# A decoder layer in fp32 on one core: the squares' fetches, the heads' factors, the lag of the second up product and the residual's stores change places

## The chip, the cores and the metric

The kernel runs on one core of a Trainium2 chip. The metric is the device time of one launch in microseconds (us), taken as the median of several runs. Before the change it is 1855.25 us, with runs between 1853.35 and 1856.14.

## The reference

One inference step of one layer: two SwiGLU blocks around a mixer. 1024 prompt tokens and 8 sample tokens go through the same weights; the sample tokens use caches for attention, convolution and pooling. All is fp32.

```python
h = h + 0.5 * swiglu(rmsnorm(h, g_f1), w_f1_gu, w_f1_down)
u = rmsnorm(h, g_mix) @ w_in          # q | k | v | conv value | conv gate | pool input
q, k = rmsnorm(q per head, g_q) * 64 ** -0.5, rmsnorm(k per head, g_k)
A = attention over three dilated windows (128,1), (512,4), (2048,16), merged by denominators
B = silu(layernorm(causal depthwise conv of width 31 over the GLU)) @ w_pw
C = trailing means over 2, 4, 8, 16 positions minus the token, a linear map per group
h = h + concat(A, B, C) @ w_out
h = h + 0.5 * swiglu(rmsnorm(h, g_f2), w_f2_gu, w_f2_down)
rmsnorm(x, g) = x * rsqrt(mean(x * x) + 1e-6) * g
```

## The kernel before

Everything is held transposed: D = 1024 features lie on the partitions (8 tiles of 128), T = 1032 token columns (1024 prompt and 8 sample) along the free axis, in two halves of 516 columns (`HF`, `HT`) and quarters of 258 (`QT`). An fp32 product is three TensorE matmuls: high part by high part, high by low, low by high. The high part of an operand is a rounded copy made by ScalarE (`hi`, L241), the low part is the remainder, a subtraction on VectorE (`lo`, L244) or, where the call says so, on GpSimd.

The stages follow each other: up 1 (`up`, L339), down 1, the mixer (projections, convolution, pooling, the v product, attention), `out_proj` (L897), up 2 and down 2. Instructions are placed on each engine by a scheduler that simulates a timeline (L1689), so an edit in one function can move instructions of others; within an engine the order is then fixed.

Up. Each up block is a Strassen-like scheme of seven products on halves, for each of the feature blocks `f`. The first products of `EARLY` blocks (14 in up 1, 12 in up 2) work on the raw x (operands `xo`, weights "11" and "12"), so they can run before the norm is known; their results are copied from PSUM by ScalarE (L521) and kept in DRAM (L522, `kept`). For one block `f` the product on the first half of the features ("11") runs first, and the product on the second half ("21") follows `lag` blocks later. Weights come by SP's queue (L465) into 8 buffers (`UP_WR`); temporaries of 128x516 (squares, copies, x) share 13 buffers (`UP_TMP`); the products share four PSUM buffers. Beside the first products runs a side generator: `norms()` squares the x of both halves (ScalarE, L405), adds the squares up (VectorE, L407), sums over the partitions by a matmul with a constant (L388), and takes the root and the reciprocal (L390, L391). `mixed()` then makes the operands of the other products (`xot`), with x fetched once more (L382). In up 2 the squares were already summed in `out_proj`, and `norms()` does only the last sum.

The first eight x tiles (half 0) come by SP's queue (L368); `fetch_x` brings the others: half 1 for the squares (the tiles named x_287 to x_293 and x_339 to x_345 in the order), and the tiles of `mixed()`.

The v loop (L1147 to L1169) makes v in 16 steps of 24 matmuls of 128x256. After each step it lets two side generators go on: `side_v`, which computes the heads' norm factors `rr` from sums of squares (L1198 to L1208, three chunks, each with a root on ScalarE and a reciprocal on VectorE), spreads them by a matmul (L1217, inside `norm(t)`) and scales q and k (L1218); and, inside `side_v`, `conv_tail`, which does the layer norm of the convolution, one chunk a step: split into high and low parts (low by GpSimd), mean by a matmul (`reduce`, L277), subtract (L1305). From the ninth v step on the generator `pre` begins the attention.

`out_proj` adds the mixer's product to the residual x tile by tile (L933), stores it to DRAM (`hd2`, L934) and squares it (L935). Its last steps already draw the first products of up 2, whose x is read back from `hd2`.

Of the kernel before, what the change touches and what calls it, by code (L numbers as in the profile page):

```python
# [11 lines left out]
F32 = mybir.dt.float32  # L12
# [8 lines left out]
KT = D // P  # L21
SEQ = 1024
NS = 8
T = SEQ + NS
# [4 lines left out]
HF = [slice(0, HT), slice(HT, T)]  # L29
HK = KT // 2  # L30
# [156 lines left out]
class Trunk:  # L187
# [151 lines left out]
    def up(self, src, n, g, norm, lag, extra=iter(())):  # L339
# [7 lines left out]
        nc = self.nc  # L347
# [8 lines left out]
        def tmp(name):  # L356
            return self.tmp.tile([P, HT], F32, tag="t", name=name)
# [19 lines left out]
            self.hi(X[i][:, 0, k], x)  # L377
            self.lo(X[i][:, 1, k], x, X[i][:, 0, k])

        def fetch_x(k, hf):  # L380
            x = tmp(f"x{hf}")
            nc.gpsimd.dma_start(x, src(k, hf))  # L382
            return x

        def total(hf, acc):
            ps = self.psp.tile([P, 2, 512], F32, tag="ps", name="ps")
            for j in range(2):
                nc.tensor.matmul(ps[:, j, 0:QT], self.mat[:, 1, :], acc[:, j * QT:(j + 1) * QT], start=True, stop=True)  # L388
            sd = tmp("sd")
            nc.scalar.activation(two(sd), ps[:, :, 0:QT], AF.Sqrt, bias=self.eps)  # L390
            nc.vector.reciprocal(self.r[:, HF[hf]], sd)  # L391

        def norms():
            if not norm:
                for _ in range(2):
                    yield
                total(1, self.tail)
                return
            accs = []
            xs = [fetch_x(k, 1) for k in range(HK)]  # L400
            for hf in range(2):
                acc = None
                for k in range(KT):
                    sq = xs[k] if hf else tmp("sq")
                    nc.scalar.activation(sq, sq if hf else first_x[k], AF.Square)  # L405
                    if k:
                        nc.vector.tensor_tensor(sq, sq, acc, op=ALU.add)  # L407
                    acc = sq
                    if k == HK - 1:
                        yield  # L410
                        if hf == 0:
                            xs += [fetch_x(i, 1) for i in range(HK, KT)]
                accs.append(acc)
                yield
            yield
            for hf in range(2):
                total(hf, accs[hf])
                yield
# [197 lines left out]
        def build(upto):  # L616
            nonlocal built
            while built < min(upto, len(order)):
                i, f = order[built]
                operand(f, OPERANDS[i][0])  # L620
                built += 1

        side = itertools.chain(norms(), mixed())
        load(0, True, "11")
        load_first(0)
# [224 lines left out]
    def body(self):  # L850
        nc, io, cst = self.nc, self.io, self.cst
        self.late = []
        self.mat = cst.tile([P, 3, P], F32, name="mat")
        nv = io["vec"].shape[1]
        self.vec = cst.tile([P, nv], F32, name="vec")
        self.eps = cst.tile([P, 1], F32, name="eps")
        self.r = cst.tile([P, T], F32, name="r")
        self.rel = cst.tile([33, 136], F32, name="rel")
        nc.vector.memset(self.r[:, 0:256], 0.0)
        nc.vector.memset(self.eps, EPS)  # L860
        nc.gpsimd.dma_start(self.mat, io["c_mat"])
        nc.gpsimd.dma_start(self.rel, io["rel"])
        self.gq = cst.tile([P, 1], F32, name="gq")
        self.ones = cst.tile([P, 2, P], F32R, name="ones")
        nc.gpsimd.tensor_copy(self.ones, self.mat[:, 1:3, :])
        self.mp = {i: [self.dr.tile([P, HT], F32, name=f"m{i}_{j}") for j in range(NP)]
                   for i in ("11", "21", "22", "t1", "t2", "t3", "t4")}
        hd, hd2 = [self.dr.tile([KT, P, T], F32, name=n) for n in ("hd", "hd2")]
        x0, x1 = io["x0"], io["x1"]
        self.late = []  # L870

        with self.first_pool() as self.x1p:
            gen = self.up(lambda k, hf: (x0, x1)[hf][:, k], 1, "g1", True, 1, self.toeplitz())
            while next(gen):
                pass
            with self.up_pools():
                for _ in gen:
                    pass
        with self.down_pools():
            self.down(1, lambda k, hf: (x0, x1)[hf][:, k],  # L880
                      lambda k, hf, x: nc.scalar.dma_start(hd[k][:, HF[hf]], x))
        nc.vector.tensor_scalar(self.gq, self.v("gq"), 0.125, None, op0=ALU.mult)
        with contextlib.ExitStack() as right:
            with self.page_pools():
                with self.side_pools():
                    mh, ml = self.mixer(hd)
                self.x1p = right.enter_context(self.first_pool())
                gen = self.up(lambda k, hf: hd2[k][:, HF[hf]], 2, "g2", False, 3)
                self.out_proj(mh, ml, hd, hd2, gen)
            with self.up_pools():  # L890
                for _ in gen:
                    pass
        with self.down_pools():
            self.down(2, lambda k, hf: hd2[k][:, HF[hf]],
                      lambda k, hf, x: nc.scalar.dma_start(io["yT"][k * P:(k + 1) * P, HF[hf]], x))

    def out_proj(self, mh, ml, hd, hd2, ahead):  # L897
        nc = self.nc
        steps = [(hf, d) for hf in range(2) for d in range(KT)]

        def load(at):
            hf, d = steps[at]
            raw = self.wrp.tile([P, T], F32, tag="wr", name="wr")
            hi, lo, x = self.pg("whi", F32R), self.pg("wlo", F32R), self.pg("h2")
            nc.sync.dma_start(raw[:, 0:D], self.io["wout"][d])
            nc.sync.dma_start(x[:, 0:HT], hd[d][:, HF[hf]])
            self.hi(hi[:, 0:D], raw[:, 0:D])
            self.lo(lo[:, 0:D], raw[:, 0:D], hi[:, 0:D])
            return hi, lo, x

        def total(hf, acc):
            for j in range(2):
                ps = self.ps()[:, 0:QT]
                c0 = hf * HT + j * QT
                nc.tensor.matmul(ps, self.mat[:, 1, :], acc[:, j * QT:(j + 1) * QT], start=True, stop=True)
                sd = self.pg("sd")[:, 0:QT]
                nc.scalar.activation(sd, ps, AF.Sqrt, bias=self.eps)
                nc.vector.reciprocal(self.r[:, c0:c0 + QT], sd)

        going = True  # L920
        nxt = load(0)
        for at, (hf, d) in enumerate(steps):
            hi, lo, page = nxt
            x, sq = page[:, 0:HT], page[:, HT:T]
            if at + 1 < len(steps):
                nxt = load(at + 1)
            for j in range(2):
                c = slice(hf * HT + j * QT, hf * HT + (j + 1) * QT)
                ps = self.ps()[:, 0:QT]
                self.mm3(ps, [(hi[:, k * P:(k + 1) * P], lo[:, k * P:(k + 1) * P], mh[k][:, c], ml[k][:, c])  # L930
                              for k in range(KT)])
                out = x[:, j * QT:(j + 1) * QT]
                nc.vector.tensor_tensor(out, ps, out, op=ALU.add)  # L933
            nc.gpsimd.dma_start(hd2[d][:, HF[hf]], x)  # L934
            nc.scalar.activation(sq, x, AF.Square)  # L935
            out = sq
            if hf and d == KT - 1:
                out = self.tail = self.wpage("tail")[:, 0:HT]
            if d:
                nc.gpsimd.tensor_tensor(out, sq, acc, op=ALU.add)  # L940
            acc = out
            if hf and d == 1:
                total(0, first)
            if d == KT - 1:
                first = acc
            if hf and going:
                going = next(ahead)
        while going:
            going = next(ahead)

    def mixer(self, hd):
        nc, io, cst = self.nc, self.io, self.cst
# [16 lines left out]
        src = [self.pg(f"h{k}") for k in range(KT)]  # L969
# [77 lines left out]
        for t in range(2):  # L1047
            wc = w[0]
            w = [unit(17)] if t == 0 else [unit(0), unit(4)]
            x = cx[t]  # L1050
# [13 lines left out]
        vs = self.mc.tile([NS, 512], F32, name="vs")  # L1064
        xs = self.mc.tile([P, KT, NS], F32, name="xs")
        for k in range(KT):
            nc.gpsimd.tensor_tensor(xs[:, k], self.xh[k][:, SEQ:T].bitcast(F32), self.xl[k][:, SEQ:T].bitcast(F32),
                                    op=ALU.add)

        def load_v(hf):  # L1070
# [20 lines left out]
        for p in range(4):  # L1091
# [7 lines left out]
            for c in range(3):  # L1099
                parts = []  # L1100
                for t, wt in zip((p, p + 4), ws):
                    x = qk[t]
# [81 lines left out]
    def side_v(self, conv, qk, acc, gq, smq):  # L1184
        nc, io = self.nc, self.io
# [17 lines left out]
        tail = self.conv_tail()  # L1203
        next(tail, None)
        yield
        for c in range(3):
            self.hi(rr[0:64, CH[c]], sc[c])
            self.lo(rr[64:128, CH[c]], sc[c], rr[0:64, CH[c]])  # L1208
        next(tail, None)
        yield  # L1210
        next(tail, None)
        yield

        def norm(t):
            for c in range(3):
# [484 lines left out]
```

## Time and profile before

| what | value |
|---|---|
| median of 3 runs | 1855.25 us (1853.35 to 1856.14) |
| the profiled execution, its own time | 1856.26 us |
| its span, first to last instruction | 1854.5 us |
| TensorE (PE) busy | 1822.7 us, 98% of the span |
| VectorE (DVE) busy | 1343.4 us, 72% |
| ScalarE (ACT) busy | 724.7 us, 39% |
| GpSimd (POOL) busy | 213.4 us, 12% |
| mean granted TensorE clock | 0.996 of full |

A row of the timeline gives the start and the length of a group of instructions in microseconds, its engine, its line, what it writes and reads, and in square brackets how long the engine had been idle before it and what it was released by. A row of the windows gives the busy time of each engine in a stretch and the clock granted to TensorE there, as a share of full speed. A row of the chain is a piece of the path that ended last: start, length, what.

### The profile page before, as it was taken

How to read it: one execution, taken by the hardware profiler on the slowest of the kernel's cores; microseconds unless marked ns; L12 is line 12 of the kernel's file. 1: busy time of each engine (PE TensorE's matmuls, PEld its weight loads, DVE VectorE, ACT ScalarE, POOL GpSimd, SP SyncE). 2: the span in 40 equal slices, each digit the busy share in tenths (PEclk: the TensorE clock that was granted, in tenths of full speed). 3: DMA queues.
4: the chain of work that ended last, by engine and by line, in shares of the span. 5: the costliest groups of instructions: out<-in, count | busy, mean ns of one | idle time of the engine just before them, and what ended most of it. 6: DMA issues, size and time to landing. Idle time of an engine off the chain costs nothing.

```text
span 1854.5 us, 35895 instructions
## 1 busy us (share of the span) xinstructions
PE 1822.7 (98%) x14436; PEld 1750.0 (94%) x14436; DVE 1343.4 (72%) x2140; ACT 724.7 (39%) x1307; POOL 213.4 (12%) x205
## 2 busy tenths in 40 slices
PE   7999999999999999999899999999999999999999
PEld 7999999999999999998865689989999999999999
DVE  6877787778686566997666755577777877868654
ACT  6532222322333455235655653443222222243342
POOL 2100000000000004732532423200000000000000
PEclk9999999999999999999999999999999999999999
DMA  9544365454964243212353256654433435596421
GB/s 330 195 139 149 115 182 191 144 183 161 327 244 118 84 158 94 53 38 75 121 159 115 93 170 207 216 169 158 131 127 111 142 120 181 168 325 245 117 81 46
DMA packets 155578, 286.72 MB, mean 155 GB/s; under 512 B 25992, under 2 KB 32732, under 8 KB 155412
## 3 DMA queue, kind: packets, MB, share of 16 engines
q1 hardware_dynamic: 116276, 206.21, 35.7%
q10 hardware_dynamic: 34560, 63.20, 9.1%
q0 software_dynamic: 4576, 15.01, 2.4%
q8 instruction: 113, 1.85, 0.4%
q14 instruction: 53, 0.43, 0.1%
HBM read 208.29 MB, written 78.61 MB: 155 GB/s over the span
## 4 chain that ended last, share of the span: by engine, by line
PE 90%; DVE 4%; DMA 3%; ACT 2%; issue 1%; SPq 0%; ACTq 0%; DVEq 0%
PE ps L512 15%; PE ps L513 15%; PE ps L514 15%; PE ps L773 8%; PE ps L774 8%; PE ps L775 8%; PE ps L283 5%; PE ps L284 5%; PE ps L285 5%; PE ps L1599 2%; PE ps L1580 1%; DMA wr<-wgu 1%; PE ps L1527 1%; DVE pt L1530 1%; PE ps L1528 1%; PE ps L1159 1%
## 5 line engine op out<-in xcount | busy, mean ns | idle before, releaser
L512 PE MATMUL ps<-xot,wop 128*128 128x258 f32 x1408 | 396.3, 283 | 1.8 <-DVE v L565 1.8
L513 PE MATMUL ps<-xot,wop 128*128 128x258 f32 x1408 | 397.9, 283 | 0.0
L514 PE MATMUL ps<-xot,wop 128*128 128x258 f32 x1408 | 397.0, 282 | 0.0
L773 PE MATMUL ps<-mop,wop 128*128 128x258 f32 x1232 | 348.1, 283 | 0.9 <-DVE v L578 0.9
L774 PE MATMUL ps<-mop,wop 128*128 128x258 f32 x1232 | 347.4, 282 | 0.0
L775 PE MATMUL ps<-mop,wop 128*128 128x258 f32 x1232 | 346.6, 282 | 0.0
L512 PE MATMUL ps<-xo,wop 128*128 128x258 f32 x1056 | 301.3, 286 | 6.1 <-ACT v L521 3.9
L513 PE MATMUL ps<-xo,wop 128*128 128x258 f32 x1056 | 300.0, 284 | 0.0
L514 PE MATMUL ps<-xo,wop 128*128 128x258 f32 x1056 | 299.6, 284 | 0.4 <-DVE wop L244 0.4
L512 PEld LDWEIGHTS ps<-xot,wop 128*128 128x128 f32 x1408 | 265.1, 189 | 2.9 <-issue 2.6
L513 PEld LDWEIGHTS ps<-xot,wop 128*128 128x128 f32 x1408 | 265.8, 189 | 1.5 <-issue 1.5
L514 PEld LDWEIGHTS ps<-xot,wop 128*128 128x128 f32 x1408 | 265.9, 189 | 0.0
L774 PEld LDWEIGHTS ps<-mop,wop 128*128 128x128 f32 x1232 | 233.5, 190 | 0.0
L773 PEld LDWEIGHTS ps<-mop,wop 128*128 128x128 f32 x1232 | 232.2, 189 | 1.1 <-issue 1.1
L775 PEld LDWEIGHTS ps<-mop,wop 128*128 128x128 f32 x1232 | 232.7, 189 | 0.0
L241 ACT ACTIVATE wop<-s 128x512 fp32r<-128x512 f32 x176 | 105.8, 628 | 292.6 <-DVE s L478 227.9
L512 PEld LDWEIGHTS ps<-xo,wop 128*128 128x128 f32 x1056 | 201.1, 191 | 9.0 <-ACT v L521 5.5
L514 PEld LDWEIGHTS ps<-xo,wop 128*128 128x128 f32 x1056 | 201.2, 191 | 0.9 <-DVE wop L244 0.8
L513 PEld LDWEIGHTS ps<-xo,wop 128*128 128x128 f32 x1056 | 201.4, 191 | 0.3 <-DVE xo L374 0.2
L244 DVE TENSOR_TENSOR wop<-wr,wop 128x512 fp32r<-128x512 f32 x180 | 121.7, 696 | 55.1 <-ACT wop L241 54.9
L244 DVE TENSOR_TENSOR wop<-s,wop 128x512 fp32r<-128x512 f32 x176 | 117.7, 688 | 36.1 <-ACT wop L241 35.6
L241 ACT ACTIVATE wop<-wr 128x512 fp32r<-128x512 f32 x180 | 107.2, 622 | 89.1 <-PE ps L775 76.7
(263 smaller groups left out, 3404.8 us busy)
## 6 DMA issues: line engine op xcount, KB each, us to landing
wr<-wgu SPq DMA_DIRECT2D x227, 256.0 KB
mt<-v ACTq DMA_DIRECT2D x88, 258.0 KB
mr<-mt SPq DMA_DIRECT2D x88, 258.0 KB
m<-v ACTq DMA_DIRECT2D x66, 258.0 KB
mr<-m SPq DMA_DIRECT2D x66, 258.0 KB
kept<-v ACTq DMA_DIRECT2D x52, 258.0 KB
v<-kept SPq DMA_DIRECT2D x52, 258.0 KB
h<-hd SPq DMA_DIRECT2D x48, 258.0 KB
```

The source lines that it names most:

```text
L241: self.nc.scalar.activation(out, src, AF.Copy)
L244: (eng or self.nc.vector).tensor_tensor(out, src, hi.bitcast(F32), op=ALU.subtract)
L283: mm(out, wh, xh, start=i == 0, stop=False)
L284: mm(out, wh, xl, start=False, stop=False)
L285: mm(out, wl, xh, start=False, stop=i == n - 1)
L512: mm(out, wh, xh, start=start and k == 0, stop=False)
L513: mm(out, wh, xl, start=False, stop=False)
L514: mm(out, wl, xh, start=False, stop=stop and k == HK - 1)
L773: mm(out, wh, mh, start=opens, stop=False)
L774: mm(out, wh, ml, start=False, stop=False)
L775: mm(out, wl, mh, start=False, stop=closes)
L1599: mm(O[half[e], q1 - w:q1], vt[j // 2][:, j % 2, hc:hc + 64], pT[:, e, :], start=j == 0, stop=j == 2 * b + 1)
```

## The change

Four edits. In `norms()` the eight fetches of x for the second half's squares are issued by SP's queue, which also carries the weights, instead of GpSimd's; `mixed()` keeps GpSimd's. In `side_v` four steps of `conv_tail` come before the first `norm(t)` instead of two. Up 2 has a lag of two blocks instead of three. The store of the residual in `out_proj` is issued by ScalarE's queue instead of GpSimd's. Beside these, eight additions of 128x8 (`xs`) go from GpSimd to VectorE.

```diff
-        def fetch_x(k, hf):
+        def fetch_x(k, hf, queue=nc.gpsimd):
             x = tmp(f"x{hf}")
-            nc.gpsimd.dma_start(x, src(k, hf))
+            queue.dma_start(x, src(k, hf))
             return x
...
-            xs = [fetch_x(k, 1) for k in range(HK)]
+            xs = [fetch_x(k, 1, nc.sync) for k in range(HK)]
...
-                            xs += [fetch_x(i, 1) for i in range(HK, KT)]
+                            xs += [fetch_x(i, 1, nc.sync) for i in range(HK, KT)]
...
-                gen = self.up(lambda k, hf: hd2[k][:, HF[hf]], 2, "g2", False, 3)
+                gen = self.up(lambda k, hf: hd2[k][:, HF[hf]], 2, "g2", False, 2)
...
-            nc.gpsimd.dma_start(hd2[d][:, HF[hf]], x)
+            nc.scalar.dma_start(hd2[d][:, HF[hf]], x)
             nc.scalar.activation(sq, x, AF.Square)
...
         for k in range(KT):
-            nc.gpsimd.tensor_tensor(xs[:, k], self.xh[k][:, SEQ:T].bitcast(F32), self.xl[k][:, SEQ:T].bitcast(F32),
+            nc.vector.tensor_tensor(xs[:, k], self.xh[k][:, SEQ:T].bitcast(F32), self.xl[k][:, SEQ:T].bitcast(F32),
                                     op=ALU.add)
...
-        next(tail, None)
-        yield
-        next(tail, None)
-        yield
+        for _ in range(4):
+            next(tail, None)
+            yield
```

On SP's queue at the start of the program, the difference (before with -, after with +); `wr<-wgu` is a weight, `x_...` a tile of x for the squares of the second half:

```order
-L465 DMA wr<-wgu 128x512 x38
+L465 DMA wr<-wgu 128x512 x9
+L382 DMA x_287<-x 128x516
+L382 DMA x_289<-x 128x516
+L382 DMA x_291<-x 128x516
+L382 DMA x_293<-x 128x516
+L382 DMA x_339<-x 128x516
+L382 DMA x_341<-x 128x516
+L382 DMA x_343<-x 128x516
+L465 DMA wr<-wgu 128x512 x2
+L382 DMA x_345<-x 128x516
+L465 DMA wr<-wgu 128x512 x27
```

Eight fetches stand among the weights now, the last of them two weights behind the others, with 27 weights behind it.

On VectorE in the same stretch, where L407 adds the squares of the second half, L244 makes the low part of a weight and L391 is the reciprocal of the first half's root; first before:

```order
L407 TENSOR_TENSOR x_339<-x_339,x_293 128x516
L244 TENSOR_TENSOR wop<-wr,wop 128x512 x2
L407 TENSOR_TENSOR x_341<-x_341,x_339 128x516
L391 RECIPROCAL r<-sd 128x516
L244 TENSOR_TENSOR wop<-wr,wop 128x512 x2
L407 TENSOR_TENSOR x_343<-x_343,x_341 128x516
L244 TENSOR_TENSOR wop<-wr,wop 128x512 x2
L407 TENSOR_TENSOR x_345<-x_345,x_343 128x516
```

and after:

```order
L407 TENSOR_TENSOR x_339<-x_339,x_293 128x516
L407 TENSOR_TENSOR x_341<-x_341,x_339 128x516
L244 TENSOR_TENSOR wop<-wr,wop 128x512
L407 TENSOR_TENSOR x_343<-x_343,x_341 128x516
L244 TENSOR_TENSOR wop<-wr,wop 128x512
L407 TENSOR_TENSOR x_345<-x_345,x_343 128x516
L244 TENSOR_TENSOR wop<-wr,wop 128x512
L391 RECIPROCAL r<-sd 128x516
```

The additions of x_343 and x_345 stood behind the reciprocal and four weight splits; now they stand ahead of the reciprocal, with two weight splits between them and x_341.

On TensorE in the v loop, a piece of the difference. L1158 to L1160 are the v product, L1164 its row factors, L277 the convolution's means, L1217 (L1216 in the new file) the spreading of the heads' factors:

```order
 L1160 MATMUL ps<-whi,xl 128x256
 L1164 MATMUL ps<-mat,r 128x1
-L1217 MATMUL ps<-rr,bcx 128x344 x3
 L277 MATMUL ps<-sh,ones 128x344
 L277 MATMUL ps<-sl,ones 128x344
@@ -6754,5 +6753,5 @@
 L1160 MATMUL ps<-whi,xl 128x256
 L1164 MATMUL ps<-mat,r 128x1
-L1217 MATMUL ps<-rr,bcx 128x344 x3
+L1216 MATMUL ps<-rr,bcx 128x344 x3
 L1158 MATMUL ps<-whi,xh 128x256
```

The piece just ahead of this one, one v step earlier, loses its L1217 rows in the same way. The first three matmuls of the heads' factors move from the row 6695 of TensorE's program to the row 6754, behind two more v steps with their conv means.

On ScalarE in up 2, where L521 copies a first product from PSUM and L522 stores it; `kept_4` and `kept_1` are the blocks 4 and 1; first before:

```order
L521 ACTIVATE v_13819<-ps 128x516
L521 ACTIVATE v_13856<-ps 128x516
L241 ACTIVATE wop<-wr 128x512 x2
L522 DMA kept_4_13066<-v_13819 128x516
L522 DMA kept_1_13063<-v_13856 128x516
```

and after:

```order
L521 ACTIVATE v_13857<-ps 128x516
L521 ACTIVATE v_13893<-ps 128x516
L241 ACTIVATE wop<-wr 128x512
L522 DMA kept_4_13066<-v_13857 128x516
L522 DMA kept_2_13064<-v_13893 128x516
```

The first product of block 4 was paired with the second of block 1, three back; now it is paired with that of block 2.

## Rows read from the trace of the kernel before

**Rows 1.** The page: busy time of each engine.

```profile
PE 1822.7 (98%) x14436; PEld 1750.0 (94%) x14436; DVE 1343.4 (72%) x2140; ACT 724.7 (39%) x1307; POOL 213.4 (12%) x205
```

**Rows 2.** TensorE's timeline, the start of up 1.

```profile
28.98 1.11 PE L388 MATMUL ps<-sq,mat 128*128 128x258 f32 x4 [1.49 <-ACT x L405]
41.58 2.06 PE L388 MATMUL ps<-x,mat 128*128 128x258 f32 x4 [5.74 <-DVE x L407]
```

**Rows 3.** Windows of the start: stretch, length, busy (instructions) by engine, granted clock.

```profile
27.50:41.60 14.10, 6.88 (x53) 6.61 (x53) 12.06 (x16) 10.54 (x19) 2.68 (x5) 0.95 0.93 320
41.60:47.10 5.50, 5.50 (x22) 5.13 (x23) 2.70 (x1) 0.69 (x1) 1.07 (x2) 0.51 0.63 199
47.10:60.00 12.90, 12.90 (x109) 12.90 (x109) 10.23 (x16) 7.22 (x14) 1.60 (x3) 1.00 0.49 164
```

**Rows 4.** VectorE's timeline at the start.

```profile
34.50 3.38 DVE L391 RECIPROCAL r<-sd 128x516 f32<-128x516 f32 x1 [1.23 <-ACT sd L390]
...
38.94 0.69 DVE L407 TENSOR_TENSOR x<-x,x 128x516 f32<-128x516 f32 x1
...
40.75 0.69 DVE L407 TENSOR_TENSOR x<-x,x 128x516 f32<-128x516 f32 x1
```

**Rows 5.** ScalarE's timeline at the start.

```profile
16.91 0.58 ACT L521 ACTIVATE v<-ps 128x516 f32<-128x516 f32 x1
...
36.93 0.63 ACT L405 ACTIVATE x<-x 128x516 f32<-128x516 f32 x1
```

**Rows 6.** Timelines of GpSimd and of SP's queue at the start.

```profile
6.67 3.71 POOL L382 DMA_DIRECT2D x<-x  x7
19.57 0.54 POOL L382 DMA_DIRECT2D x<-x  x1 [9.20 <-DVE sq L407]
...
1.21 4.25 SPq L368 DMA_DIRECT2D x<-x  x8
```

**Rows 7.** The chain that ended last, at the start: two weights on their way.

```profile
8.75 10.15 DMA wr<-wgu
...
32.69 4.33 DMA wr<-wgu
```

**Rows 8.** Timelines of VectorE and TensorE: last write and first use of xot.

```profile
95.85 0.70 DVE L244 TENSOR_TENSOR xot<-x,xot 128x516 fp32r<-128x516 f32 x1
...
99.76 0.28 PE L512 MATMUL ps<-xot,wop 128*128 128x258 f32 x1
```

**Rows 9.** TensorE's timeline, the heads' factors in the v loop.

```profile
886.62 0.66 PE L1217 MATMUL ps<-rr,bcx 128*128 128x344 f32 x1 [3.98 <-DVE rr L244]
```

**Rows 10.** Windows of the v loop.

```profile
882.60:886.80 4.20, 0.21 (x2) 0.18 (x1) 4.14 (x7) 1.89 (x5) 2.02 (x4) 0.98 0.01 3
886.80:893.60 6.80, 5.26 (x20) 4.53 (x21) 4.60 (x8) 3.67 (x7) 3.76 (x4) 0.51 0.27 94
```

**Rows 11.** The chain in the v loop: the means of one convolution step.

```profile
896.11 0.63 PE ps L277 x4
```

**Rows 12.** Timelines of VectorE and GpSimd in the v loop.

```profile
869.64 0.93 DVE L1084 TENSOR_TENSOR few<-few 8x256 f32<-8x256 f32 x2 [5.85 <-ACT few L1082]
...
888.90 0.51 DVE L244 TENSOR_TENSOR rr<-stat,rr 64x344 fp32r<-64x344 f32 x1
...
886.70 1.20 POOL L244 TENSOR_TENSOR sl<-cy,sh 128x344 fp32r<-128x344 f32 x1 [2.12 <-ACT v L1166]
```

**Rows 13.** TensorE's timeline, the start of up 2.

```profile
1186.07 0.39 PE L512 MATMUL ps<-xo,wop 128*128 128x258 f32 x1 [0.94 <-ACT wop L241]
...
1204.58 0.39 PE L512 MATMUL ps<-xo,wop 128*128 128x258 f32 x1 [0.45 <-ACT v L521]
...
1250.16 0.39 PE L512 MATMUL ps<-xo,wop 128*128 128x258 f32 x1 [0.69 <-ACT v L521]
```

**Rows 14.** The chain at the start of up 2: the last store, then the operands.

```profile
1176.37 5.96 DMA hd<-h
1182.44 2.58 ACT xo L373 x4
```

## The prediction

> **What bounds the kernel now.** I read the busy times first: TensorE works 98% of the span, so some 32 us in all are idle, and of the other engines none is near its limit [rows 1]. Nothing can be won except where TensorE stands still or runs at a lower clock. So I went along TensorE's timeline for rows with a bracket, and by the windows for stretches with a granted clock below 1. Three places hold most of it.
>
> At the start of up 1, TensorE waits 1.49 us for the sum of the first half's squares and 5.74 us for that of the second [rows 2]. After the second wait the granted clock is 0.51 of full, the lower of its two levels (1.2 of 2.4 GHz), for 5.50 us [rows 3]. In the v loop it waits for the heads' factors: 3.98 us before the first spreading matmul [rows 9], and by the windows 3.99 us of 4.20 are idle and then 1.54 of 6.80, 5.53 in all. There too the 6.80 us behind the wait are granted only 0.51 [rows 10]. At the start of up 2, eight second products, one each 6.5 us, wait 0.45 us (the last 0.69) for ScalarE's copy of a first product, and the very first product waits 0.94 us [rows 13].
>
> **Edit 1, the start.** The wait of 5.74 us is not for a transfer. The last tile, x_345, was fetched at 19.57 [rows 6], but ScalarE squared it at 36.93 [rows 5], and VectorE added it last at 40.75, behind the reciprocal of the first half (3.38 us from 34.50) and four weight splits [rows 4]. What counts is the order on these engines. In the new order ScalarE reaches that square after 13 weight splits instead of 18, and VectorE has the last three adds ahead of the reciprocal.
>
> When is the sum ready then? SP issues a transfer in 0.53 us (8 in 4.25), and GpSimd takes as long (7 in 3.71) [rows 6]. The fetches stand behind nine weights; the ninth goes out near 14 us, seven fetches follow until about 18, and x_345 waits for a temporary, freed by the first adds of squares near 20 (GpSimd's fetch had waited for just that until 19.57). With the slowest landing among the rows, 10.15 us [rows 7], x_345 is there by 30.2; its square (0.63) and its add (0.69) make 31.5, and a weight split or two ahead of them 33.4 at most. TensorE comes to that matmul at 41.58 − 5.74 − 1.49 = 34.35. So the 5.74 goes. With it goes the slow stretch: 5.50 us at 0.51 do the work of 2.8, a loss of 5.50 × 0.49 = 2.7. The 1.49 is less sure: ScalarE's last square of the first half has 20 instructions ahead of it since the first copy (16.91 before [rows 5]) instead of 18, but weights no longer share the transfers with GpSimd's seven fetches at 6.67, so this copy comes up to 4 us earlier. Between 0 and 1.49 I take half, 0.75. Term: 5.74 + 2.7 + 0.75 = **9.2**.
>
> What is late next: the operands `xot` of `mixed()`. Before, the last was written at 95.85 + 0.70 = 96.5, and first used at 99.76 [rows 8], 3.2 us of slack. TensorE moves forward by about 10, VectorE's chain by some 8.5 (its second reciprocal starts when the sum is there, near 34.5 instead of 43.6), so the slack shrinks to about 2 and holds. The transfers of `mixed()` stay on GpSimd. Weights behind the fetches: 13 are ahead of them or between, enough for TensorE until about 6.3 + 5.9 + 12 × 2.84 + 2 = 48, where 24 matmuls take 24 × 12.90/109 = 2.84 us [rows 3].
>
> **Edit 2, the v loop.** Two v steps (2 × 2.84) and two sets of means (2 × 0.63 [rows 11]) come before the first spreading matmul: 6.9 us of work that does not need the factors. TensorE, there at 886.62 − 3.98 = 882.64, is now there at 889.6. The third chunk's factor was written at 888.90 + 0.51 = 889.41 [rows 12]; one chunk's subtraction is now ahead of it on VectorE, about 0.2 us more than the multiplication it replaces, and the third matmul comes half a us behind the first. So 5.53 of idle go, and of the 5.26 us busy at 0.51 the loss of 5.26 × 0.49 = 2.6. Term: **8.1**. Queued behind: from the ninth step the attention's first part needs scaled heads; the first two are done at the sixth and seventh step, a step ahead still.
>
> **Edit 3, lag 2.** With lag 3 a second product starts when all four PSUM buffers hold something: it must wait until ScalarE has copied the first product that ended just before. With lag 2 one pair is free at this moment. Term: 7 × 0.45 + 0.69 = **3.85**. Cost: the second half's x is needed one product (2.84) earlier.
>
> **Edit 4, the stores by ScalarE's queue, and `xs`.** The last store lies on the chain: 5.96 us from issue to landing, then the operands of up 2 [rows 14]. At best the 0.94 us wait goes, at worst nothing changes; I take 0.5. The instruction behind each store on ScalarE, the square of the same tile, needs the same addition of VectorE, so the new wait holds nothing up; 16 issues of about 0.5 us are hidden on an engine 39% busy [rows 1]. The Trainium skill ("DMA: Bandwidth & Descriptors", "Specifications") gives a transfer started by ScalarE some 0.4 us less latency than one started by GpSimd; by that alone the term would be 0.4, an estimate from that page, and no row here shows it. The `xs` additions cost VectorE at most 8 × 0.47 us (two larger ones take 0.93 [rows 12]); a single one stands between operands, so between 0 and 0.5 us reach TensorE.
>
> Against this stand waits that a new order makes elsewhere; such waits have 0.45 to 0.94 us now [rows 13]. Between 0 and 4 of them, I take −**1.5** with `xs`.
>
> Sum: 9.2 + 8.1 + 3.85 + 0.5 − 1.5 = 20.2. The profiled execution takes 1856.26 (span 1854.5 and 1.8 around it), so 1836.1 on its scale; it lies 1.0 above the median, so **1835.0**. With everything full and no new wait: 9.9 + 8.1 + 3.85 + 0.9 = 22.8, 1832.5.
>
> **Rivals.**
> A: the start gains nothing. The squares now hang on a queue full of weights: if the fetches land only as a weight did among the x tiles, 10.15 us against 4.33 alone [rows 7], and every one of them more than once in turn, ScalarE and VectorE, which work in order, stand still, and the wait is as long as before. For it: 0.93 of the transfers' capacity is taken in that stretch [rows 3]. Against it: the sum would have to come 8 us later than my 33.4. Time: 20.2 − 9.2 = 11.0, 1844.2. The Trainium skill ("DMA: Bandwidth & Descriptors", "Issuing engines are not separate DMA queues") says that another issuer saves issuing time only, since all transfers run on the same 16 engines; the equal 0.53 us of rows 6 says that there is not even that to save. By that rule the queue alone would give this rival; the new order on VectorE is what speaks against it.
> B: `xot` becomes late. If VectorE's chain doesn't move, TensorE waits until 96.5 and runs slowly after it: of the 9.2, 3.2 − 2.7 = 0.5 stay, 1843.7.
> C: the v wait moves to the third mean. It needs a low part that GpSimd wrote at 886.70 + 1.20 = 887.9 [rows 12]; TensorE is there at 882.64 + 0.63 + 2.84 = 886.1. A wait of 1.8, and 2.6 if the clock falls again: 1839.4. Against it: GpSimd had waited there 2.12 us for ScalarE, which is freer now.
> D: in up 2 the second half's x is late by one product, 2.84: 1837.8.
> E: no change to be measured. The start as in A, and in the v loop the work moved ahead delays the factors by as much (a gain of nothing in place of 8.1): 1852.3.
> F: slower. SP's queue is in order: if x_345's fetch is held there for a temporary, 27 weights stand behind it. GpSimd's queue was held 9.20 us for the same fetch [rows 6], where nothing stood behind. A fetch held until t gives a weight at t + 4.33 and its split 1.3 later, against 48 on TensorE; with the slow clock behind it the whole gain is gone if t passes 48 + 20.2 − 2.7 − 5.6 = 60, say 1858. Against it: the temporary comes free near 20.
>
> **How the numbers follow.** Forecast 0.52; A 0.10, B 0.10, C 0.10, D 0.06, E 0.06, F 0.06. What a measurement can tell from no change is 0.2%, 3.7 us. All but E and F lie beyond it: faster 0.88, same 0.06, slower 0.06. The range runs from 1830.5 (everything full, and 1.9 as the lowest run of before lies below its median) to 1845.5 (A, with 1.3 for its uncertainty); E and F lie outside, and a part of A.
>
> **What would show it.** Right: no wait before the second set of L388, no stretch at a clock of 0.51 near 42 to 47 and 887 to 894, no wait before L1216, none for ScalarE's copy in up 2. Wrong: a wait in front of L388 (A), of the first xot (B), of L277 (C), of the first "21" product of up 2 (D), or an idle TensorE near 48 with SP's queue held at an x fetch (F).

## The result

The changed kernel takes 1828.64 us (median of 4 runs, 1827.21 to 1831.58), before 1855.7 us (1853.35 to 1856.7): a ratio of 0.9858, with an interval of 0.9841 to 0.9875. Run again on another occasion it took 1829.41 us, a ratio of 0.9858 (0.9845 to 0.9872). It is some 27 us faster where 20 were forecast, and 1.9 us below the low end of the range.

### The profile page after: what moved, and what is told of

Read it like the earlier page. It is cut to its first block, busy times and chain, and to the rows that moved or that the text cites. A ratio compares the mean times of both kernels' runs of the same rounds, so it can differ in the third digit from the quotient of the medians.

```text
span 1829.7 us, 35859 instructions
## 1 busy us (share of the span) xinstructions
PE 1813.4 (99%) x14436; PEld 1743.9 (95%) x14436; DVE 1343.5 (73%) x2148; ACT 723.8 (40%) x1307; POOL 191.0 (10%) x173
## 4 chain that ended last, share of the span: by engine, by line
PE 92%; DVE 3%; DMA 2%; ACT 1%; issue 1%; SPq 0%; ACTq 0%; DVEq 0%
PE ps L512 15%; PE ps L513 15%; PE ps L514 15%; PE ps L773 8%; PE ps L775 8%; PE ps L774 8%; PE ps L283 5%; PE ps L284 5%; PE ps L285 5%; PE ps L1598 2%; PE ps L1579 1%; PE ps L1526 1%; PE ps L1158 1%; PE ps L1159 1%; PE ps L1160 1%
## 5 line engine op out<-in xcount | busy, mean ns | idle before, releaser
L244 DVE TENSOR_TENSOR wop<-wr,wop 128x512 fp32r<-128x512 f32 x180 | 121.0, 693 | 49.0 <-ACT wop L241 48.7
L244 DVE TENSOR_TENSOR wop<-s,wop 128x512 fp32r<-128x512 f32 x176 | 117.6, 688 | 37.1 <-ACT wop L241 36.6
```

Of the source, the lines that this page charges most:

```text
L244: (eng or self.nc.vector).tensor_tensor(out, src, hi.bitcast(F32), op=ALU.subtract)
```

## The profile after

Its page: span and busy times.

```profile
span 1829.7 us, 35859 instructions
...
PE 1813.4 (99%) x14436; PEld 1743.9 (95%) x14436; DVE 1343.5 (73%) x2148; ACT 723.8 (40%) x1307; POOL 191.0 (10%) x173
```

The span is 24.8 us shorter; TensorE has the same 14436 instructions and is busy 9.3 us less. Most of this lies at the start and in the v loop, where stretches at the lower clock are gone; but 2.3 us of it (447.03 against 444.77 busy) lie between the end of `out_proj` and the last first product of up 2, where the granted clock is 1.00 in both traces. They are near the 8 × 0.26 us by which the waits there cost more than their brackets, told with edit 3 undone. The profiled execution's own time is 1831.58, the longest of its four, where that of before was near its median. So 24.7 us of the 27.1 between the medians can be looked for in these two traces; the other 2.4 come from how far these two executions lie above their medians (2.9 and 0.6 us).

TensorE's timeline: at the start (both sets of L388), in the v loop, and at the start of up 2.

```profile
27.94 1.11 PE L388 MATMUL ps<-sq,mat 128*128 128x258 f32 x4 [1.04 <-ACT v L521]
34.41 1.03 PE L388 MATMUL ps<-x,mat 128*128 128x258 f32 x4
428.84 0.39 PE L512 MATMUL ps<-xot,wop 128*128 128x258 f32 x1 [0.70 <-DVE v L565]
881.43 0.73 PE L1216 MATMUL ps<-rr,bcx 128*128 128x344 f32 x3
1168.02 0.39 PE L514 MATMUL ps<-xo,wop 128*128 128x258 f32 x1 [0.23 <-DVE wop L244]
```

Beside [rows 2] the 5.74 us have no bracket any more, and the 1.49 are 1.04, now released by a copy out of PSUM (L521) and no longer by a square (L405). Beside [rows 9] the three spreading matmuls run in one piece. Of [rows 13] none of the waits for L521 is left, nor the 0.94. The row at 428.84 is a new one.

What stands behind the 1.04 is in the chain that ended last. ScalarE has a store of a first product to issue (L522; ACTq is its queue). By the chain the store comes only when a fetch of x on SP's queue has landed, near 22.3, and the squares and copies behind it on ScalarE come later by as much:

```profile
15.87 6.47 DMA x<-x
...
22.42 0.33 ACTq L522
...
22.80 1.16 ACT sq L405 x2
```

The windows that answer to [rows 3] and [rows 10], and one over the first products of up 2:

```profile
34.40:41.60 7.20, 7.20 (x59) 7.09 (x58) 7.20 (x6) 4.22 (x9) 1.61 (x3) 1.00 0.98 338
41.60:47.10 5.50, 5.50 (x48) 5.50 (x47) 5.50 (x9) 2.61 (x5) 0.00 (x0) 1.00 1.00 368
881.40:893.60 12.20, 12.20 (x94) 11.88 (x95) 9.36 (x15) 8.87 (x22) 6.61 (x8) 1.00 0.45 151
1168.00:1232.00 64.00, 63.98 (x533) 63.98 (x534) 57.06 (x87) 40.52 (x72) 5.35 (x10) 1.00 0.77 262
```

TensorE is not idle and the granted clock is 1.00 in all of them: 48 matmuls run between 41.60 and 47.10 where 22 did.

VectorE's timeline at the start, beside [rows 4]:

```profile
29.76 0.69 DVE L407 TENSOR_TENSOR x<-x,x 128x516 f32<-128x516 f32 x1
30.37 0.68 DVE L244 TENSOR_TENSOR wop<-wr,wop 128x512 fp32r<-128x512 f32 x1
31.17 0.70 DVE L407 TENSOR_TENSOR x<-x,x 128x516 f32<-128x516 f32 x1
31.78 0.69 DVE L244 TENSOR_TENSOR wop<-wr,wop 128x512 fp32r<-128x512 f32 x1
33.69 3.38 DVE L391 RECIPROCAL r<-sd 128x516 f32<-128x516 f32 x1 [1.22 <-ACT sd L390]
...
39.33 3.37 DVE L391 RECIPROCAL r<-sd 128x516 f32<-128x516 f32 x1
...
90.99 0.69 DVE L244 TENSOR_TENSOR xot<-x,xot 128x516 fp32r<-128x516 f32 x1
```

The last add ends at 31.9, within the 31.5 to 33.4 forecast, and ahead of the reciprocal; TensorE comes at 34.41. The last two rows are the second half's reciprocal and the last write of `xot`, in up 1, for the account at the end.

Where the 24.8 us come from, as the difference of the start of the same matmul in both traces:

| stretch | before, after | gain in it |
|---|---|---|
| to the first `xot` product | 99.76, 90.20 | 9.56 |
| to the first row factor of the v loop (L1164) | 871.61, 862.53 | −0.48 |
| to the end of the v loop (L1174) | 939.72, 922.29 | 8.35 |
| to up 2 (last L285 of `out_proj`) | 1175.33, 1157.71 | 0.19 |
| to the last first product (`xo`) of up 2 | 1628.02, 1603.34 | 7.06 |
| to the last matmul | 1850.18, 1825.43 | 0.07 |

## The experiments

Twelve runs, each timed in several rounds beside the kernel before on the same chip. Ratios are to that; the times lost are counted from the changed kernel's 1829.41.

**The changed kernel again** (no edit).

> The changed kernel once more, on the chip on which its undone parts run, as their measure. Theory: the 27.1 us between the medians are 24.7 us that the two profiled executions show place by place (9.5 at the start, 8.4 in the v loop, 7.1 in up 2, -0.2 elsewhere) and some 2.4 us of scatter from run to run, so the ratio to before comes out between 0.985 and 0.988 (gain 22 to 28 us), and the profile repeats the places. Rival: the profiled execution of the change was a bad one and the gain is really 27 or more, in a place the profile didn't show: then the new profile differs from the old one by 2 to 3 us at some place.

1829.41 us, 0.9858 (0.9845 to 0.9872). By the same stretches: 9.67, 0.59, 8.35, 1.0, 7.08, 0.08. So the three places repeat within 0.15 us, and this execution is 2.0 us shorter between them: the row at 428.84 isn't there, and the stretch with the attention gains 0.8 more. The ratio is the theory's. The rival had one thing right: the first profiled execution was a long one, and this one shows 26.8 us of gain by the spans. There is no fourth place.

**Edit 1 undone.**

```diff
-            xs = [fetch_x(k, 1, nc.sync) for k in range(HK)]
+            xs = [fetch_x(k, 1) for k in range(HK)]
...
-                            xs += [fetch_x(i, 1, nc.sync) for i in range(HK, KT)]
+                            xs += [fetch_x(i, 1) for i in range(HK, KT)]
```

> The changed kernel with the squares' fetches back on GpSimd's queue, the other edits kept. Theory (the order on VectorE and ScalarE, which the scheduler draws up from the queue, makes the wait): the wait of about 5.7 us in front of the second set of L388 and the stretch at half clock behind it come back, and the kernel loses about 9.5 us of its gain. Rival (rival A of the prediction: the queue counts for nothing, the start's gain came by other edits that moved the schedule): it loses under 2 us.

1841.94 us, 0.9925 (0.9912 to 0.9939): 12.5 us lost. TensorE's timeline of it at the two sets of L388:

```profile
29.09 1.11 PE L388 MATMUL ps<-sq,mat 128*128 128x258 f32 x4 [1.85 <-DVE sq L407]
41.97 2.06 PE L388 MATMUL ps<-x,mat 128*128 128x258 f32 x4 [6.02 <-DVE x L407]
```

The window behind the second wait:

```profile
41.90:47.40 5.50, 5.43 (x21) 5.09 (x22) 2.61 (x1) 0.69 (x1) 1.07 (x2) 0.50 0.68 216
```

Wait and half clock are back, so rival A is out. The first `xot` product starts at 100.34, 10.1 us after that of the changed kernel. In the traces the whole loss is 10.2 us against the changed kernel's first execution and 12.2 against its second, so what the medians show beyond the 10.1 isn't settled place by place; a wait of 1.32 us at the mixer's start, 0.71 in the changed kernel, is back and has a part of it.

**Edit 1 alone, on the kernel before.** The diff is the one above reversed, with the new argument of `fetch_x`.

> The kernel before with the squares' fetches on SP's queue and nothing else changed. Theory: the start's gain stands by itself, 9.5 to 11.6 us by the first xot as in the changed kernels' profiles, and up to 1 us more behind it: 10 to 12.5 us, a ratio of 0.9933 to 0.9946. Rival: the 12.5 us lost by the undone edit hold 2 us or more that come only with the other edits; 9.5 us or less are won.

1844.0 us, 0.9942 (0.9928 to 0.9955): 11.3 us won. The first `xot` product starts at 88.55, 11.2 us before that of the kernel before. The edit stands by itself.

**Half of edit 1: the last four fetches by GpSimd again.**

```diff
-                            xs += [fetch_x(i, 1, nc.sync) for i in range(HK, KT)]
+                            xs += [fetch_x(i, 1) for i in range(HK, KT)]
```

> The changed kernel with the last four of the squares' fetches back on GpSimd's queue, the first four on SP's. The scheduler then puts the last add (x_345) right behind the reciprocal instead of ahead of it; the other adds stay ahead. Theory (the order decides): the sum is ready only after the reciprocal, and TensorE waits 2 to 4 us before the second set of L388, with a slower clock behind it if it is near 4; 2 to 6 us are lost against the changed kernel. Rival (the queue decides): the last fetch, issued by GpSimd, lands early enough, no wait, under 1 us lost.

1834.11 us, 0.9886 (0.9873 to 0.99): about 5 us lost. VectorE's timeline of it, the reciprocal and the last add:

```profile
34.19 3.38 DVE L391 RECIPROCAL r<-sd 128x516 f32<-128x516 f32 x1 [1.15 <-ACT sd L390]
37.49 0.63 DVE L407 TENSOR_TENSOR x<-x,x 128x516 f32<-128x516 f32 x1
```

TensorE's timeline, the second set of L388:

```profile
38.27 1.36 PE L388 MATMUL ps<-x,mat 128*128 128x258 f32 x4 [3.03 <-DVE x L407]
```

The last add stands right behind the reciprocal and ends when that and itself are done; TensorE waits 3.03 us, and the clock in the 7.8 us behind is 0.78. The order decides, as the theory had it. In the kernel before, the reciprocal was a part only: the square of x_345 ended at 37.56 there [rows 5], so with VectorE free the sum would still have come some 2.4 us after TensorE (an estimate: 37.56 and an add of 0.69, against 41.58 − 5.74 = 35.84).

**The fetches by ScalarE's queue.**

```diff
-            xs = [fetch_x(k, 1, nc.sync) for k in range(HK)]
+            xs = [fetch_x(k, 1, nc.scalar) for k in range(HK)]
...
-                            xs += [fetch_x(i, 1, nc.sync) for i in range(HK, KT)]
+                            xs += [fetch_x(i, 1, nc.scalar) for i in range(HK, KT)]
```

> The changed kernel with the squares' fetches issued by ScalarE's queue. The scheduler then puts all adds of the second half ahead of the reciprocal too, as with SP's queue. Theory (the order on the engines that work in order makes the start, not the queue): no wait in front of the second set of L388, the time within 2 us of the changed kernel's 1829.4. Rival (SP's queue is what helps): the wait of 5.7 us is back, 1839 to 1842.

1835.82 us, 0.9889 (0.9875 to 0.9904), between the two. TensorE's timeline, the first set of L388:

```profile
30.40 1.47 PE L388 MATMUL ps<-sq,mat 128*128 128x258 f32 x4 [4.32 <-ACT v L521]
```

The windows ahead of it and behind it:

```profile
26.00:30.40 4.40, 0.08 (x2) 0.01 (x1) 4.40 (x8) 4.40 (x10) 0.00 (x0) 1.00 1.02 360
30.40:34.00 3.60, 3.60 (x15) 3.28 (x16) 3.29 (x6) 3.58 (x7) 1.60 (x3) 0.59 0.88 247
```

The second wait is gone without SP's queue, as the theory says of it. But the first set now waits 4.32 us for a copy by ScalarE (L521), which is busy all the time in that wait, and the clock falls behind it too. The total came out 6 us above the changed kernel, where 2 were allowed: the theory looked at one wait only.

**Edit 2 undone.**

```diff
-        for _ in range(4):
+        for _ in range(2):
             next(tail, None)
             yield
```

> The changed kernel with two steps of the convolution ahead of the heads' factors again instead of four. Theory: TensorE waits about 4 us for rr again, with 6.8 us at half clock behind it, and 8.4 us are lost. Rival: part of the v loop's gain is the xs additions' or the start's shift, and 5 us or less are lost.

1837.42 us, 0.9904 (0.989 to 0.9917): 8.0 us lost. TensorE's timeline, the first spreading matmul:

```profile
874.76 0.65 PE L1216 MATMUL ps<-rr,bcx 128*128 128x344 f32 x1 [3.32 <-DVE rr L244]
```

The window from there:

```profile
874.70:882.00 7.30, 5.70 (x21) 4.97 (x22) 4.80 (x9) 3.67 (x7) 4.13 (x4) 0.50 0.29 98
```

The v loop gains −0.15 us here, and 8.25 to 8.44 in the kernels with four steps. The whole stretch hangs on this edit.

**Edit 3 undone.**

```diff
-                gen = self.up(lambda k, hf: hd2[k][:, HF[hf]], 2, "g2", False, 2)
+                gen = self.up(lambda k, hf: hd2[k][:, HF[hf]], 2, "g2", False, 3)
```

> The changed kernel with a lag of three blocks in up 2 again. Theory: each of the eight waits costs more than the idle time in its bracket, because the first matmul behind it starts later than the stream would have it: 0.72 us each where the bracket says 0.45, so 6.0 us are lost, and the other 1.1 us of up 2's gain (its start) stay. Rival 1: the brackets are the price, 3.85 us are lost. Rival 2: the start of up 2 hangs on the lag too, 7.1 us are lost.

1834.71 us, 0.989 (0.9876 to 0.9903): 5.3 us lost by the medians. In its trace up 2 gains 0.88 us over before, where the changed kernel gains 7.06: 6.18 us. The brackets of its eight waits add up to 3.91. TensorE's timeline around one of them:

```profile
1187.75 0.28 PE L514 MATMUL ps<-xo,wop 128*128 128x258 f32 x1
1188.63 0.39 PE L512 MATMUL ps<-xo,wop 128*128 128x258 f32 x1 [0.61 <-ACT v L521]
1188.86 0.28 PE L513 MATMUL ps<-xo,wop 128*128 128x258 f32 x1
1188.97 0.28 PE L514 MATMUL ps<-xo,wop 128*128 128x258 f32 x1
```

In the stream one matmul starts 0.12 us after the other. Here 0.88 us pass, and then 0.23 before the next: 0.76 + 0.11 = 0.87 us lost where the bracket says 0.61. The bracket counts from the end of the last matmul (it lasts 0.28, though in the stream the next starts after 0.12), and the first matmul behind takes longer (0.39). This adds 0.26 to the wait. The other seven, read by their starts in the same way, show 0.26 or 0.27, and 3.91 + 8 × 0.26 = 6.0.

**Edit 3 alone, on the kernel before** (lag 3 to 2, nothing else).

> The kernel before with a lag of two blocks in up 2 and nothing else changed. Theory: the eight waits go and each is worth the 0.69 us by which the matmul behind it starts later than the stream would have it, not the 0.45 us of its bracket; with what follows each, 5.3 to 6.2 us are won, a ratio of 0.9967 to 0.9971. Rival: the brackets are the price, 3.85 us, 0.9979.

1850.93 us, 0.9973 (0.9962 to 0.9983), 4.3 us by the medians. The interval holds both prices, so the times don't decide. The trace does: from the end of `out_proj` to the last first product 5.96 us are won, within the theory's 5.3 to 6.2.

**Lag 1.**

```diff
-                gen = self.up(lambda k, hf: hd2[k][:, HF[hf]], 2, "g2", False, 2)
+                gen = self.up(lambda k, hf: hd2[k][:, HF[hf]], 2, "g2", False, 1)
```

> The changed kernel with a lag of one block in up 2. Theory: the second product of a block then runs one product (2.84 us) behind the first, and the copy between them takes 0.6 us, so no wait comes back and the time stays within 1 us of the changed kernel. Rival: the second half's x, which comes last from out_proj, is needed another product earlier and is late, 1 to 3 us are lost at the start of up 2.

1834.24 us, 0.9885 (0.9871 to 0.9898). About 5 us are lost by the medians. The rival is right about the place. TensorE's timeline:

```profile
1162.78 0.39 PE L512 MATMUL ps<-xo,wop 128*128 128x258 f32 x1 [1.83 <-ACT wop L241]
...
1178.91 0.39 PE L512 MATMUL ps<-xo,wop 128*128 128x258 f32 x1 [1.21 <-ACT v L521]
```

The start of up 2 waits 1.83 us: by the chain the last store of the residual lands there first, then ScalarE makes the operands from the x read back (2.58 us), a copy and this weight. And against the theory a wait for a copy (L521) comes back once, of 1.21 us. The stretch gains 3.98 us instead of 7.06; what the medians show beyond these 3.1 us isn't placed.

**Edit 4 undone: the stores by GpSimd.**

```diff
-            nc.scalar.dma_start(hd2[d][:, HF[hf]], x)
+            nc.gpsimd.dma_start(hd2[d][:, HF[hf]], x)
```

> The changed kernel with the residual's stores back on GpSimd's queue; TensorE's instructions stand in the same order. Theory: the first product of up 2 hangs on the last store, and 0.5 to 1.1 us are lost there (with ScalarE's queue the stage gained 0.87 us even at a lag of three). Rival: the stores count for nothing, the 0.87 us come from the order of the operands on ScalarE, and the time stays within 0.5 us.

1830.58 us, 0.9863 (0.9848 to 0.9878): not to be told from the changed kernel by its time. Its chain at the last store:

```profile
1158.41 5.36 DMA hd<-h
```

The same of the changed kernel:

```profile
1158.49 5.06 DMA hd<-h
```

Up 2 gains 6.5 us instead of 7.06, with a wait of 0.36 us in front of its first product that the changed kernel doesn't have. That the stores are the reason is not shown: with ScalarE's stores kept, such a wait stands in two other traces (0.47 us with edit 2 undone, 0.41 with more matmuls on zeros), and in the eight traces with lag 2 and ScalarE's stores up 2 gains between 6.25 and 7.56 us. What the traces do show is a shorter way to the operands of up 2: from the start of the last addition (L933) to the first of them (L373) 6.19 to 6.79 us pass in the four kernels with GpSimd's stores, and 4.94 to 6.32 in the ten traces with ScalarE's.

**The `xs` additions on GpSimd again.**

```diff
-            nc.vector.tensor_tensor(xs[:, k], self.xh[k][:, SEQ:T].bitcast(F32), self.xl[k][:, SEQ:T].bitcast(F32),
+            nc.gpsimd.tensor_tensor(xs[:, k], self.xh[k][:, SEQ:T].bitcast(F32), self.xl[k][:, SEQ:T].bitcast(F32),
```

> The changed kernel with the eight xs additions back on GpSimd; TensorE's instructions stand in the same order. Theory: nothing to be measured, under 0.5 us either way, at most a row at the start of the mixer (0.71 us now, 1.32 before) that changes. Rival: the additions on VectorE are what shortened that wait, and 0.6 us are lost.

1828.52 us, 0.9854 (0.9839 to 0.9869), the same as the changed kernel. The wait at the mixer's start is 0.71 us here too, so its fall from 1.32 isn't the additions' doing. It mostly goes with edit 1 (0.71 with edit 1 alone, 1.32 with edit 3 alone or edit 1 undone), but the next kernel has 1.34 with it.

**More matmuls on zeros at the start.**

```diff
-AHEAD, WARM = 5, 4
+AHEAD, WARM = 5, 6
```

> The changed kernel with six matmuls on zeros at the very start instead of four (they show as eight and twelve rows of L644). In the profiles the first products run at half speed, 0.215 us between matmuls, until 10.5 to 12.6, after TensorE stood idle 1.3 to 2.3 us before the first product; what differs from run to run there is what differs between profiles of one kernel. Theory: a TensorE that is kept busy up to the first product doesn't fall to the lower clock, the products run at 0.12 us from the start, and 1 to 2.5 us are won. Rival: the first products are paced by the operands, or the matmuls on zeros push the first product back; the time stays or grows by up to 1 us.

1831.44 us, 0.9866 (0.9849 to 0.9882): nothing won. The clock does what the theory says: the first products start 0.12 us apart from 9.10 on, where the other traces have 0.21 until 10.0 to 12.8. But the first product starts at 6.54, no earlier than elsewhere, and the first set of L388 at 25.64, without a wait, only 0.36 us before the earliest of the other traces. A wait of 1.21 us at 46.05, which no other trace has, takes more than that. Whether the start alone would be worth something in the time stays open.

None of the twelve beats the changed kernel by more than the measurement can tell.

## Why the prediction was wrong, point by point

The direction, the three places and what ends the wait at each were right; the size was too small: 20.2 us forecast, 24.7 in the two profiled executions, 27.1 between the medians. The 4.5 us between the first two are 2.7 in up 2, 1.2 in waits that did not come, 0.4 at the start and 0.3 in the v loop.

- **The term of edit 3 failed: 3.85 us, and 6.0 to 6.2 measured** (5.96 alone, 6.18 undone). The sum took the brackets as the price of the waits; each of these waits costs about 0.26 us more than its bracket, and there are eight. So the term was 2.1 to 2.3 us too small, and the whole of up 2, with its start, came to 7.06 instead of 4.35. Its risk, x needed a product earlier (rival D), did not come at lag 2; at lag 1 it did.
- **The deduction of 1.5 us for new waits** was −0.3 in the changed kernel's first trace (a new wait of 0.70 us near 428, another shorter by 0.6) and a gain of 1.6 in the second: 1.2 us or more too pessimistic, and the place where two traces of one kernel differ most. The rows gave what one such wait takes now; how many there would be was a guess.
- **Edit 1: 9.2 forecast, 9.56 in the trace.** The parts: 1.04 up to the first set of L388 (0.75 taken), 6.13 between the two sets (5.74), 2.39 behind (2.7). That this agrees so well is partly luck. With all eight fetches on SP's queue seven other kernels reach the first `xot` product 10.3 to 11.6 us earlier than before, and the 11.3 us of median for edit 1 alone say that this is nearer to its worth. The first set of L388 starts at 28.98 to 29.23 in the three traces without the edit and at 25.64 to 27.94 in the nine with all of it. The 1.49 us wait can go entirely: six of the nine have no wait there. The three that have one (1.04, 1.48 and 1.30 us, the changed kernel in both its traces and the one with edit 4 undone) are the three in which ScalarE stood idle 1.4 to 1.6 us until the fetch of x named above had landed, at 21.6 to 22.3; in the other six it had landed at 19.5 to 20.6, and ScalarE stood 0.17 us at most. So a late fetch among the weights, what rival A feared, did come in part, and cost about 1 us. Some of the rest lies before: in the three traces without the edit TensorE waits 0.16 to 0.77 us for weights near 15 and 16, in the nine it doesn't. The prediction gave a half of the 1.49 for this, with the reason that GpSimd's fetches no longer share the transfers at 6.67; the rows fit it, but no run tests that reason by itself.
- **What is late next was misread.** VectorE's chain was to move forward by 8.5 us, with the second reciprocal near 34.5. It starts at 39.33 (44.40 before), behind four weight splits, and the last `xot` is written at 91.68, only 4.9 us before the 96.55 of [rows 8]. That is 1.5 us after the first `xot` product starts (90.20), so the 2 us of slack were not there. Rival B did not come all the same: the first matmuls on `xot` ran before that write, and those that follow, at 93.44, did not wait either. Which of them reads this tile isn't settled here.
- **Edit 2: 8.1 forecast, 8.35 measured.** The last of the factors was ready at 881.03 (the row below), 0.4 us before TensorE came at 881.43; 0.2 were forecast. VectorE's timeline:

```profile
879.87 1.16 DVE L244 TENSOR_TENSOR rr<-stat,rr 64x344 fp32r<-64x344 f32 x1
```

- **Edit 4: 0.5 forecast.** The traces differ by 0.6, which is within what up 2 differs by from kernel to kernel; `xs` was worth nothing that can be measured.
- **The range** ended at 1830.5 because "everything full" was 22.8, built on brackets, with 1.9 for scatter. With 7.06 for up 2, 8.35 for the v loop and the 11.3 of edit 1 alone, full is 26.7 us, which is 1828.6 from 1855.3: the measured 1828.64.
- Rivals B, C, E and F did not come, and A only as told above: no wait of TensorE at the first `xot` (90.20) or at L277, and none near 48. What rival A draws from the Trainium skill ("DMA: Bandwidth & Descriptors", "Issuing engines are not separate DMA queues") agrees with the traces as far as it goes: the second wait goes with ScalarE's queue as with SP's. The gain of the start lies in the order that the scheduler draws up from the queue.

## What to carry to other kernels

Where an engine is busy 98% of the time, list its idle rows, and price each by the starts of the instructions on both sides against the stream's own spacing, not by the bracket; add what the windows show of a lower clock behind it. When a move of a transfer changes a static order, look for what the order does to the engines that work in sequence, above all for long instructions (a reciprocal of 3.38 us) that land ahead of a short one that others wait for. And see how far a stage's time moves between executions before a range is set: a profiled execution that is long among its own hides part of a gain.

## What the runs showed that was not expected

- Between a wait's bracket and its price lie 0.26 us for matmuls of 258 columns (0.61 and 0.87 at one wait; over eight waits 3.91 of brackets, and 6.18 in the stage).
- What a wait costs in clock behind it did not simply grow with its length: 3.03 us left a granted clock of 0.78 over 7.8 us, 4.32 us one of 0.59 over 3.6 us and 1.00 from then on, and 3.3, 4.0, 5.7 and 6.0 us one of 0.50 or 0.51 over 5.5 to 7.3 us.
- The start of the same instructions differs by 2 us between traces: the first set of L388 starts at 26.00 with edit 3 undone and at 27.94 in the changed kernel. In the one the fetch of x lands at 20.2 and ScalarE does not stand, in the other at 22.3, and the set waits 1.04 us; the first product starts at 6.26 and 7.23.
